# Modulation columns of five groups as GpSimd sums of scaled weight rows instead of 32-column TensorE matmuls

## The chip, the cores and the metric

One core of one Trainium2 chip runs the whole program as one launch. The metric is device time in microseconds (us) from one launch, the median of several runs. The engines named below are TensorE (PE, with its weight loads PEld), VectorE (DVE), ScalarE (ACT), GpSimd (POOL) and SyncE (SP), which issues every DMA of this kernel.

## The reference, cut to what matters

Two transformer layers run over 1024 latent tokens, with 256 context tokens as a prefix. Each layer is steered by modulation columns: a vector-matrix product of a conditioning vector with a weight of 1024 x 6144, once for the latents (`mod`) and once for the context (`mod_c`).

```python
s_c, s_cc = silu(c), silu(c_ctx)
for l in range(2):
    need_ctx = l < 1
    mod   = s_c  @ ada_w[l] + ada_b[l]          # 6144 columns, latents
    mod_c = s_cc @ ada_w[l] + ada_b[l]          # 6144 columns, context
    sh1, sc1, g1, sh2, sc2, g2 = split(mod, 6)  # the same for mod_c
    h  = rms_norm(x,  norm_g[l, 0]) * (1 + sc1) + sh1
    hc = rms_norm(xc, norm_g[l, 0]) * (1 + csc1) + csh1
    y, yc = mixer(h, hc)                        # even: windowed and latent attention
    x = x + g1 * rms_norm(y, norm_g[l, 1])      # odd: normalised and differential attention
    h = rms_norm(x, norm_g[l, 2]) * (1 + sc2) + sh2
    x = x + g2 * rms_norm(swiglu(h), norm_g[l, 3])
    if need_ctx:                                # the context goes through the same steps
        ...
```

In layer 1 the context is normalised for the mixer (which needs `csh1` and `csc1`), and nothing else of `mod_c` is read there.

## The kernel before, in words

Activations lie feature-major: 128 features on the partitions, tokens along the row. Large products are made of float32r matmuls on halves hi and lo of each operand. Work is laid out in program order on a `Recorder`, which stands in place of the engines. At the end `Recorder.issue` lists the instructions anew: an engine that is free in its estimate takes, of the instructions whose operands are there, the first in program order, and a tile is given out ahead of earlier ones only when enough buffers stay free for those (`room`). After that each engine's list is fixed, and the hardware works through each list strictly in order; a wait of one row holds every row behind it on that engine. The scratch tiles are few: 44 of type `T` (128 x 1024), 13 of type `U` (128 x 512), 24 small ones `S`, 8 PSUM banks `b`.

The modulation columns of a layer come in three groups of 2048 columns (g = 0, 1, 2). `g_ada(l, g)` loads the weight in 8 blocks of 128 rows (`kt`), two `T` tiles each. For every block it issues four matmuls (`q`), with the block's 32 columns of `silc` as stationary operand (two of them used, silu(c) and silu(c_ctx), the others zero) and 512 weight columns as moving operand, in float32. Four results of 32 rows share one PSUM bank. Then ScalarE copies the bank, four transposes turn it, and VectorE adds the bias into `mod[l]`; `derive` makes the scales and gates of it.

Group (0, 0) is made at the very start, since the first norm waits for it. The other five are put in a slow queue, `pr.slow`, of which `tick` advances one step per slot of attention. Groups (0, 1), (0, 2), (1, 0) enter at the start of layer 0's attention, groups (1, 1), (1, 2) at the start of layer 1's.

Attention is run by `run_jobs`, slot by slot: a slot is one piece of scores (a PSUM bank), its maximum on VectorE, the exponentials of a piece before on ScalarE (`ex`), and a share of the products with the values (`pv_steps`: transposes, hi and lo copies in two `U` tiles, products). Layer 0 has 352 score pieces: 144 of windowed attention, called A here, then 208 of latent attention, called B. Layer 1 has 192 pieces of differential attention, D, then 192 of normalised attention, C. GpSimd has a part in each. In A and B it adds the two halves of a head pair in `fin` (`T<-T,U`, after a DMA has moved one half), splits the outputs, and copies and adds small columns. In D it combines the two streams of each query tile (`combine`): two products with a factor broadcast along the row (`T<-T,S`) and two sums (`T<-T,T`) of 128 x 512, after which those weights are transposed and multiplied with the values.

The lines that set this:

```python
for q in range(4):
    self.mm(ps[32 * q:32 * q + 32, :], self.silc[:, kt, :],
            ws[kt][q // 2][:, (q % 2) * 512:(q % 2) * 512 + 512], kt == 0, kt == KT - 1)
    yield
# tick():
if self.slow and next(self.slow[0], self) is self:
    self.slow.popleft()
# combine(), on GpSimd:
for h in (slice(0, 512), slice(512, 1024)):
    pr.tt(pb1[:, h], pb1[:, h], f.to_broadcast([P, 512]), ALU.mult, eng=nc.gpsimd)
    pr.tt(pb[:, h], pb[:, h], pb1[:, h], ALU.add, eng=nc.gpsimd)
```

Of the kernel before, what the change touches and what calls it, by code (L numbers as in the profile page):

```python
# [19 lines left out]
P = 128  # L20
D = 1024
# [11 lines left out]
# columns of the packed per-partition parameters  # L33
# [3 lines left out]
# steps from transposed probabilities to their products; slots from differential scores to their weights  # L37
LAG, ALAG, DLAG = 3, 2, 10
# weight tiles split ahead of their products: in layer 0's and layer 1's mixers and output projections
NEAR, ONEAR, N1 = 1, (3, 1), 3  # L40
# time that the pieces of the work beside the matmuls take or wait, us
# [9 lines left out]
class Recorder:  # L51
    """Stands for nc while the program is laid out. The instructions are then issued as a list schedule orders them:
    an engine that is free takes, of the instructions whose operands are there, the first in program order.
    Times are estimates that only decide the order; Tile sets every wait."""
# [26 lines left out]
    @staticmethod  # L81
    def boxes(ap):
        """Tile name and the boxes (rows, columns) that ap covers."""
        shape = ap.tensor.shape
        w = 1
        for s in shape[1:]:
            w *= s
        r0, c0 = divmod(ap.offset, w)
        rows, cols, twice = 1, 1, 0
        for stride, n in ap.ap:  # L90
            if n == 1:
                continue
            if stride >= w:
                rows += (n - 1) * (stride // w)
            elif n == 2 and stride > 512:
                twice = stride
            else:
                cols += (n - 1) * stride
        out = [(r0, r0 + rows, c0, c0 + cols)]
        if twice:  # L100
            out.append((r0, r0 + rows, c0 + twice, c0 + twice + cols))
        return out
# [25 lines left out]
    def record(self, k, f, name, args, kw):  # L128
# [23 lines left out]
        if k == 0:  # L152
            # products into one bank stay in order: a first one marks the whole bank
            t = outs[0].tensor.name
            if t in self.bank:
                deps.add(self.bank[t])
            self.bank[t] = i
        self.ops.append((k, f, name, args, kw, deps, tiles, self.cost(k, name, outs[0], ins, kw), i + self.bias))

    def issue(self):  # L160
# [14 lines left out]
        # from the engine of the row to the engine of the column  # L175
# [87 lines left out]
class FM:  # L263
    """Feature-major activations of one token chunk: [128, KT, n] over 4 KB tiles."""
# [11 lines left out]
class Prog:  # L276
# [41 lines left out]
    def tick(self, us=2.0, wide=1):  # L318
        """Stages of the work under way beside us microseconds of matmuls: one of all short pieces, of the first
        long ones as many as that time has room for, and one of the slow queue.  # L320
        A long piece yields the time that a stage takes, or less than 0 for a time to wait."""
        for g in list(self.bg):
            if next(g, self) is self:
                self.bg.remove(g)
        self.now += us
        self.credit = min(self.credit + us, CAP)
        while self.credit > 0:
            e = next((e for e in list(self.seq)[:wide] if e[1] <= self.now), None)
            if e is None:
                break  # L330
            t = next(e[0], self)
            if t is self:
                self.seq.remove(e)
            elif t < 0:
                e[1] = self.now - t
            else:
                self.credit -= t
        if self.slow and next(self.slow[0], self) is self:
            self.slow.popleft()
# [56 lines left out]
    def split(self, x, hi, lo):  # L396
        """x (float32) into hi + lo, both float32r, exactly."""
        self.nc.scalar.copy(hi, x)
        self.sub(lo, x, f32(hi))
# [4 lines left out]
    def mm3(self, ps, terms):  # L404
        """sum over terms (whi, wlo, xhi, xlo) of w^T x."""
# [6 lines left out]
    def wsplit(self, raw, w=1024):  # L412
        """The first w columns of a weight tile, split."""
        hi, lo = self.T(F32R), self.T(F32R)
        self.split(raw[:, :w], hi[:, :w], lo[:, :w])
        return hi, lo

# [19 lines left out]
    def g_ada(self, l, g, ahead=2):  # L437
        """The 2048 modulation columns of group g."""
# [37 lines left out]
    def derive(self, l, g):  # L476
        """Scales and gates with the norms' gains: A1, G1, A2, G2 per feature and stream."""
        def gain(i):
            c0 = C_NG + (l * 4 + i) * 8
            return self.par[:, c0:c0 + 8].unsqueeze(2).to_broadcast([P, 8, 2])  # L480
        m, dr = self.mod[l], self.der[l]
# [9 lines left out]
    def rstd(self, acc, n, dim, g=1, eng=None):  # L491
        """1/sqrt(mean + eps) per token from the sums acc, each [128, n] (to be added, and over partitions).
        g=2: partitions 0-63 and 64-127 are summed apart. Columns [128 tokens, g] per token tile."""
# [12 lines left out]
        # first guess from the exponent, then three Newton steps  # L506
# [8 lines left out]
    def expand(self, cols):  # L515
        """Columns [128, w], each 64 times in a row."""
# [5 lines left out]
    def bcast(self, cols, g=1):  # L522
        """Token columns [128, nt * g] to rows: [128, n tokens] in PSUM."""
# [8 lines left out]
    def sq_add(self, acc, x, n, k):  # L532
        """x^2, the k-th term, to the sums acc (one on Pool, a second one on DVE)."""
# [17 lines left out]
    def g_modnorm(self, x, n, A, Bv, put, acc=None, w=1):  # L551
        """rms-normalised x times A plus B, split; A(kt), B(kt) are per-partition columns."""
# [20 lines left out]
    def g_residual(self, y, acc, src, G, acc2):  # L573
        """x + G * rms(y), in y's place; x comes from DRAM; its squares' sum goes to acc2."""
# [34 lines left out]
    def load_fm(self, src, c):  # L609
        """src: DRAM [1024 features, tokens of the chunk]."""  # L610
# [16 lines left out]
    def rope(self, q, cos, sin, half, rows=P, n=512):  # L627
        """q [rows, n] float32 in place."""
# [12 lines left out]
    def later(self, f, ticks=2):  # L641
        """f, some ticks later."""
# [8 lines left out]
    def split_out(self, q, dst, c, r0, eng=None, done=None):  # L651
        """q float32 to hi and lo and on to the scratch: dst [rows, 2, tokens], from row r0 on."""
# [20 lines left out]
    def run_jobs(self, jobs):  # L673
        """Slot by slot: one piece of scores, one piece of the step before to its exponentials, and a share
        of the products with the values for the jobs before."""
# [54 lines left out]
class Proj:  # L730
    """Feature-major products with weight tiles that stream through.
    wsrc: DRAM weight tiles [128, KT*M]; order: (tile, chunk) pairs; evac(tile, chunk, psum)."""
# [59 lines left out]
class Job:  # L792
    """One head (or differential head), up to four query tiles.
    passes(si, qi): list of (lhsT, rhs(kind, a, b)) of stream si, kind 'x' or 'c' keys;
    vt(kt): list of (values, 'h' or 'hl' parts of the probabilities, first and last query tile);
    sinks: list of (head, first and last query tile)."""
# [16 lines left out]
    def delay(self):  # L813
        """Slots until the last probabilities are there."""
        return 0 if self.neglam is None else DLAG

    def s_steps(self):
        """Per query tile and stream: score pieces (each returns its maximum's work) and exponentials."""
# [73 lines left out]
    def combine(self, qi, pb1, pc1, s):  # L892
        """p0 - lam z0 / z1 p1, in p0's place: z0 times the differential weights."""
# [15 lines left out]
    def sums(self):  # L909
        """The sums of the exponentials, one column per query tile."""  # L910
# [23 lines left out]
    # windowed  # L934
# [32 lines left out]
    def pcol(self, qi, kt):  # L967
        """probabilities of query tile qi on key tile kt (8, 9: context)."""
# [74 lines left out]
def even_mixer(pr, h, OT, pre_out):  # L1043
    """Layer 0: windowed attention with sinks (A) and latent attention (B), outputs to OT [1024, tokens].
    A generator: first what can be had before the norm."""
# [99 lines left out]
    # latent up-projections  # L1145
# [117 lines left out]
    pr.slow.extend(pr.g_ada(l, g) for l, g in ((0, 1), (0, 2), (1, 0)))  # L1263
# [5 lines left out]
class Pair:  # L1269
    """An even and an odd head that share one 128-row tile of the output: their epilogues.  # L1270
    Products with the values come as [main | low] rows for the even head and [low | main] for the odd one."""
# [10 lines left out]
    def rout(self, c, e=None):  # L1282
        """Where the reciprocal sums of head e (None: of both, context) go."""
# [51 lines left out]
def odd_mixer(pr, h, OT, pre_out):  # L1335
    """Layer 1: normalised grouped attention (C) and differential attention (D), outputs to OT [1024, SEQ].
    A generator: first what can be had before the norm."""
# [5 lines left out]
    # lambda  # L1343
# [79 lines left out]
    # values, token-major  # L1423
# [51 lines left out]
    for hd in range(4):  # L1475
        for c, i0 in (("a", 0), ("b", 4)):
# [30 lines left out]
            elif hd == 0:  # L1507
                loadf = lambda: pr.slow.extend(pr.g_ada(1, g) for g in (1, 2))
# [18 lines left out]
def load_dup(pr, src, r0):  # L1527
    """Keys of one head, hi and lo, each on both halves of the partitions."""
# [15 lines left out]
class OutFFN:  # L1544
    """Output projection, residual, norm, SwiGLU and its residual for the chunks of layer l."""
# [34 lines left out]
    def g_pre(self):  # L1580
        """While attention ends: the first weights, and the attention outputs chunk by chunk."""
# [29 lines left out]
    # SwiGLU, hidden tile by hidden tile  # L1611
# [155 lines left out]
def rope_tables(dim, half):  # L1767
    """cos and signed sin [128, SEQ] for heads of dim rows, two axes, half frequencies each."""
# [22 lines left out]
def columns(w):  # L1791
    """[1024, n*128] to n contiguous tiles [128, KT*128]."""
# [4 lines left out]
def layout(i):  # L1797
    """The inputs in the order in which the kernel reads them."""
# [53 lines left out]
```

## Time and profile before

| | |
|---|---|
| median of 3 runs | 3406.78 us (3404.93 to 3407.7) |
| span of the profiled execution | 3405.7 us, first to last instruction (its time around the span is not on the page) |
| busy: PE, PEld | 3302.8 us (97%), 2687.9 us (79%) |
| busy: DVE, ACT, POOL | 2079.6 us (61%), 1398.0 us (41%), 697.2 us (20%) |
| attention of layer 0 | about 245 us to 740 us of the span |
| attention of layer 1 | about 2060 us to 2545 us |

A busy share is a mean over stages with different limits, and matmuls are pipelined with modelled ends, so PE at 97% is not PE at its peak. All instructions have one source line (L260, the recorder's), so groups are told apart by their tiles: `b` is a PSUM bank, `T<-T,U` an instruction that writes a `T` tile and reads a `T` and a `U` tile.

### The profile page before, as it was taken

The page shows a single profiled execution, that of the slowest core. Times are in us where ns is not written, and L with a number is a line of the kernel's source. Part 1 is how long each engine was busy: PE and PEld are TensorE (multiplying, and loading weights), DVE is VectorE, ACT ScalarE, POOL GpSimd, SP SyncE. Part 2 cuts the span into 40 slices and gives each one's busy share as a digit, 9 for nine tenths or more (in the row PEclk, how much of TensorE's full clock was granted, in tenths as well). Part 3 has the DMA queues.
Part 4 walks back from the last instruction along what each step waited for, and adds up shares of the span by engine and source line. Part 5 has one row for each costly group of instructions (what it writes and reads, how often), then busy time and mean ns, then how long its engine had stood idle before and what let it go on. Part 6 is the DMA issues. An engine that isn't in the chain of part 4 may idle for free.

```text
span 3405.7 us, 45603 instructions
## 1 busy us (share of the span) xinstructions
PE 3302.8 (97%) x16916; PEld 2687.9 (79%) x16916; DVE 2079.6 (61%) x4013; ACT 1398.0 (41%) x3200; POOL 697.2 (20%) x1059
## 2 busy tenths in 40 slices
PE   7989999999999999999998999999999999999997
PEld 5865588887888888888877895678887788888886
DVE  5565588875534444444468745898994545444545
ACT  4365688874411111111134324788994411111111
POOL 2311221125200000000044723682114200000003
PEclk8999999999999999999999999999999999999998
DMA  6266442354201111111123346412145211111111
GB/s 236 81 236 229 167 132 72 98 193 160 80 28 42 44 38 38 38 38 38 38 95 136 105 133 194 130 52 71 60 163 176 68 56 38 56 43 51 56 56 62
DMA packets 134446, 325.56 MB, mean 96 GB/s; under 512 B 12432, under 2 KB 34640, under 8 KB 134224
## 3 DMA queue, kind: packets, MB, share of 16 engines
q1 hardware_dynamic: 134224, 322.65, 28.8%
q8 instruction: 133, 2.18, 0.3%
q14 instruction: 89, 0.73, 0.1%
HBM read 243.63 MB, written 71.63 MB: 93 GB/s over the span
## 4 chain that ended last, share of the span: by engine, by line
PE 82%; DVE 8%; POOL 3%; DMA 3%; ACT 2%; issue 2%; POOLq 0%; SPq 0%; DVEq 0%; ACTq 0%
PE b L260 82%; DVE T L260 3%; DVE U L260 3%; DVE S L260 2%; POOL S L260 2%; POOL U L260 1%; ACT T L260 1%; DMA scr<-T 1%; ACT U L260 1%; DMA T<-in_ada_w_dram 1%; DMA U<-scr 1%; POOL T L260 0%; DMA T<-in_ctxT_dram 0%; POOLq L1847 0%; DMA T<-scr 0%
## 5 line engine op out<-in xcount | busy, mean ns | idle before, releaser
L260 PE MATMUL b<-T,T 128*128 128x512 f32 (+5 forms) x9958 | 2170.5, 367 | 23.1 <-DVE T L260 9.6
L260 PEld LDWEIGHTS b<-T,T 128*128 128x128 f32 (+2 forms) x9958 | 1714.3, 190 | 378.9 <-issue 27.9
L260 PE MATMUL b<-U,T 128*128 128x512 f32 (+2 forms) x3808 | 946.0, 381 | 9.4 <-DVE U L260 4.4
L260 PEld LDWEIGHTS b<-U,T 128*128 128x128 f32 x3808 | 661.6, 190 | 135.6 <-issue 12.8
L260 POOL TENSOR_TENSOR U<-U,U 128x512 f32<-128x512 f32 (+1 forms) x130 | 174.9, 1349 | 1696.5 <-ACT U L260 1692.2
L260 DVE TENSOR_TENSOR T<-T,b 128x512 f32<-128x512 f32 (+1 forms) x872 | 501.6, 631 | 11.4 <-PE b L260 6.5
L260 DVE TENSOR_TENSOR T<-T,T 128x1024 fp32r<-128x1024 f32 (+4 forms) x274 | 316.7, 1170 | 227.3 <-PE b L260 172.9
L260 DVE TENSOR_REDUCE S<-b 128x1 f32<-128x512 f32 (+1 forms) x672 | 377.3, 571 | 116.2 <-PE b L260 111.0
L260 DVE TENSOR_TENSOR U<-U,b 128x512 f32<-128x512 f32 (+1 forms) x118 | 75.2, 637 | 608.4 <-PE b L260 605.5
L260 ACT ACTIVATE T<-b,S 128x512 f32<-128x512 f32 (+1 forms) x640 | 390.6, 616 | 53.5 <-DVE S L260 36.0
L260 ACT CAST T<-T 128x1024 fp32r<-128x1024 f32 (+4 forms) x234 | 225.1, 968 | 360.8 <-PE b L260 296.4
L260 DVE TENSOR_TENSOR U<-b,U 128x512 fp32r<-128x512 f32 (+3 forms) x528 | 335.6, 648 | 21.2 <-ACT U L260 16.8
L260 ACT ACTIVATE U<-b 128x256 f32<-128x256 f32 (+1 forms) x148 | 81.3, 552 | 620.8 <-PE b L260 618.8
L260 ACT CAST U<-b 128x512 fp32r<-128x512 f32 (+3 forms) x528 | 295.7, 572 | 97.4 <-PE b L260 90.4
L260 PE MATMUL b<-ident,T 128*128 128x128 f32 x1968 | 314.3, 276 | 6.3 <-DVE U L260 2.5
L260 PEld LDWEIGHTS b<-ident,T 128*128 128x128 f32 x1968 | 239.7, 141 | 76.0 <-ACT T L260 9.3
L260 ACT CAST U<-U 128x512 fp32r<-128x512 f32 (+1 forms) x110 | 63.6, 578 | 305.1 <-DVE U L260 300.9
L260 POOL TENSOR_TENSOR T<-T,T 128x512 f32<-128x512 f32 (+2 forms) x104 | 132.5, 1282 | 175.6 <-ACT T L260 162.4
L260 PE MATMUL b<-T,silc 128*32 128x512 f32 x384 | 131.8, 626 | 11.0 <-DMA T<-in_ada_w_dram 10.5
L260 DVE TENSOR_TENSOR U<-U,U 128x512 fp32r<-128x512 f32 (+4 forms) x167 | 118.9, 713 | 38.2 <-POOL U L260 27.1
L260 ACT ACTIVATION_READ_ACCUMULATOR T<-b,S 128x1 f32 x640 | 136.6, 213 | 0.0
L260 ACT ACTIVATE U<-T 128x512 f32<-128x512 f32 (+1 forms) x174 | 96.4, 578 | 96.1 <-DVE T L260 90.4
(71 smaller groups left out, 1514.5 us busy)
## 6 DMA issues: line engine op xcount, KB each, us to landing
scr<-T SPq DMA_DIRECT2D x114, 512.0 KB
T<-in_ada_w_dram SPq DMA_DIRECT2D x96, 512.0 KB
T<-in_ffn_in_dram SPq DMA_DIRECT2D x88, 512.0 KB
T<-scr SPq DMA_DIRECT2D x82, 512.0 KB
T<-scr SPq DMA_DIRECT2D x88, 256.0 KB
T<-in_ffn_out_dram SPq DMA_DIRECT2D x44, 512.0 KB
T<-in_w_out_dram SPq DMA_DIRECT2D x32, 512.0 KB
T<-scr SPq DMA_DIRECT2D x72, 128.0 KB
```

The lines of the kernel that those rows point to most:

```text
L260: f(*args, **kw)
```

## The change

Groups (0, 1), (0, 2), (1, 0), (1, 1), (1, 2) are made by a new generator, `g_ada_pool`; group (0, 0) stays with `g_ada`. Each group is made in two halves of 1024 columns. For a half, the 8 weight blocks are loaded into one `T` tile each. GpSimd multiplies each block by its per-partition scalar of `silc` (`TENSOR_SCALAR`, 128 x 512) and adds the products up in an accumulator tile `acc[v]` (`TENSOR_TENSOR`, 128 x 512), for `nv` conditioning vectors: two, or one for groups (1, 1) and (1, 2), whose context columns nothing reads. At the end of a half, 8 float32 products per vector, with 128 columns of `acc[v]` as stationary operand and a column of ones as moving operand, sum over the partitions into one PSUM bank, and VectorE adds the bias. The slow queue advances by one scaled half row block per slot.

```diff
+    def g_ada_pool(self, l, g):
+        nc, d, gp = self.nc, self.d, self.nc.gpsimd
+        nv = 2 if l == 0 or g == 0 else 1
+        m = self.mod[l]
+        for i in range(2):
+            c0 = g * 2048 + i * 1024
+            ws = {}
+
+            def load(kt):
+                if kt < KT:
+                    ws[kt] = self.T()
+                    self.load(ws[kt], d["ada_w"][l, kt * P:(kt + 1) * P, c0:c0 + 1024])
+
+            load(0)
+            load(1)
+            yield
+            acc = [self.T() for _ in range(nv)]
+            for kt in range(KT):
+                w = ws.pop(kt)
+                for v in range(nv):
+                    sc = self.silc[:, kt, v:v + 1]
+                    for h in (slice(0, 512), slice(512, 1024)):
+                        if kt:
+                            t = self.U()
+                            self.ts(t, w[:, h], sc, eng=gp)
+                            self.tt(acc[v][:, h], acc[v][:, h], t, ALU.add, eng=gp)
+                        else:
+                            self.ts(acc[v][:, h], w[:, h], sc, eng=gp)
+                        yield
+                load(kt + 2)
+            yield
+            ps = self.b()
+            for q in range(8):
+                for v in range(nv):
+                    self.mm(ps[:, 2 * q + v:2 * q + v + 1], acc[v][:, q * P:(q + 1) * P], self.ones[:, 0:1], True, True)
+            c1 = g * 16 + i * 8
+            pv = ps[:, 0:16].rearrange("p (q v) -> p q v", v=2)[:, :, 0:nv]
+            bv = self.par[:, C_AB + l * 48 + c1:C_AB + l * 48 + c1 + 8].unsqueeze(2).to_broadcast([P, 8, nv])
+            self.add(m[:, c1:c1 + 8, 0:nv], pv, bv)
+        self.derive(l, g, nv)
...
-    pr.slow.extend(pr.g_ada(l, g) for l, g in ((0, 1), (0, 2), (1, 0)))
+    pr.slow.extend(pr.g_ada_pool(l, g) for l, g in ((0, 1), (0, 2), (1, 0)))
...
-                loadf = lambda: pr.slow.extend(pr.g_ada(1, g) for g in (1, 2))
+                loadf = lambda: pr.slow.extend(pr.g_ada_pool(1, g) for g in (1, 2))
```

`derive` takes `nv` and works on so many columns; the other differences are comments.

How the lists change is seen at three places. The first is GpSimd's list where layer 0's attention begins. `S_538` is a small column of the first job; `U_452` a tile of the latent projections. Before:

```order
L260 TENSOR_TENSOR U_452<-U_452,T_113 128x512
L260 COPY S_538<-S_537 128x4
L260 COPY S_756<-par 128x4
L260 TENSOR_TENSOR S_538<-S_538 128x4
L260 COPY U_608<-S_512 128x256
```

Now, with `T_545` and `T_546` the two accumulators of the first half and `T_542`, `T_543` its first weight blocks:

```order
L260 TENSOR_TENSOR U_452<-U_452,T_113 128x512
L260 TENSOR_SCALAR T_545<-T_542,silc 128x512 x2
L260 TENSOR_SCALAR T_546<-T_542,silc 128x512 x2
L260 TENSOR_SCALAR U_560<-T_543,silc 128x512
L260 TENSOR_SCALAR U_566<-T_543,silc 128x512
L260 TENSOR_TENSOR T_545<-T_545,U_560 128x512
L260 TENSOR_TENSOR T_545<-T_545,U_566 128x512
L260 TENSOR_SCALAR U_568<-T_543,silc 128x512
L260 TENSOR_SCALAR U_571<-T_543,silc 128x512
L260 TENSOR_TENSOR T_546<-T_546,U_568 128x512
L260 COPY S_538<-S_537 128x4
L260 TENSOR_TENSOR T_546<-T_546,U_571 128x512
```

The job's own copy now stands behind eleven large instructions of the new kind. In all, 360 such instructions (192 `TENSOR_SCALAR`, 168 `TENSOR_TENSOR`) stand in GpSimd's list between the start of layer 0's attention and its score piece 221, with 98 of the attention's own between them.

The second place is TensorE's list in layer 0. Before, in A, rows with `silc` stand singly between score products (`T_877,T_878`, `T_875,T_878`, `T_876,T_878`) and transposes of weights (`ident`):

```order
L260 MATMUL b_975<-T_956,silc 32x512
L260 MATMUL b_983<-T_877,T_878 128x256 x2
L260 MATMUL b_975<-T_957,silc 32x512 x2
L260 MATMUL b_984<-T_875,T_878 128x384
L260 MATMUL b_984<-T_876,T_878 128x384
L260 MATMUL b_986<-T_877,T_878 128x256 x2
```

Now, in B, the sums of the sixth and last half of layer 0 (`b_1811`, accumulators `T_1599` and `T_1600`) stand between score products and transposes, near score piece 221:

```order
L260 MATMUL b_1896<-T_1658,T_1656 128x512
L260 MATMUL b_1896<-T_1659,T_1656 128x512
L260 MATMUL b_1896<-T_1658,T_1657 128x512
L260 MATMUL b_1897<-ident,T_1834 128x128
L260 MATMUL b_1897<-ident,T_1848 128x128
L260 MATMUL b_1897<-ident,T_1861 128x128
L260 MATMUL b_1897<-ident,T_1882 128x128
L260 MATMUL b_1811<-ones,T_1600 128x1
L260 MATMUL b_1811<-ones,T_1599 128x1
```

The rows with `silc`, the last of which stood near score piece 100, are gone; the rows with `ones` wait for GpSimd's last addition into their accumulator, and stand near the pieces 46, 74, 109, 143, 185 and 221, one half each.

The third place is GpSimd's list in D. Before, the four large instructions of `combine` follow one another query tile by query tile, with nothing but a small copy between:

```order
L260 TENSOR_TENSOR T_4200<-T_4200,S_4194 128x512 x2
L260 TENSOR_TENSOR T_4195<-T_4195,T_4200 128x512 x2
L260 COPY S_4172<-S_4219 128x1
L260 TENSOR_TENSOR T_4231<-T_4231,S_4219 128x512 x2
L260 TENSOR_TENSOR T_4220<-T_4220,T_4231 128x512 x2
```

Now, with `T_4423` an accumulator and `T_4479`, `T_4487` weight blocks:

```order
L260 TENSOR_TENSOR T_4473<-T_4473,S_4452 128x512 x2
L260 TENSOR_TENSOR T_4453<-T_4453,T_4473 128x512 x2
L260 TENSOR_SCALAR U_4488<-T_4479,silc 128x512
L260 TENSOR_SCALAR U_4492<-T_4479,silc 128x512
L260 TENSOR_TENSOR T_4423<-T_4423,U_4488 128x512
L260 TENSOR_TENSOR T_4423<-T_4423,U_4492 128x512
L260 TENSOR_SCALAR U_4497<-T_4487,silc 128x512
L260 TENSOR_SCALAR U_4499<-T_4487,silc 128x512
L260 TENSOR_TENSOR T_4423<-T_4423,U_4497 128x512
L260 TENSOR_TENSOR T_4423<-T_4423,U_4499 128x512
L260 COPY S_4466<-S_4489 128x1
L260 TENSOR_TENSOR T_4500<-T_4500,S_4489 128x512 x2
```

Between two query tiles' combinations stand eight rows of the new kind. All 120 of layer 1 (64 `TENSOR_SCALAR`, 56 `TENSOR_TENSOR`) stand before score piece 74 of D's 192, with 68 of D's own rows; the four halves' rows with `ones` stand near D's pieces 15, 33, 53 and 73.

## Rows read from the trace of the kernel before

**Rows 1.** The page: busy time, and two of the rows in 40 slices.

```profile
PE 3302.8 (97%) x16916; PEld 2687.9 (79%) x16916; DVE 2079.6 (61%) x4013; ACT 1398.0 (41%) x3200; POOL 697.2 (20%) x1059
...
PE   7989999999999999999998999999999999999997
...
PEclk8999999999999999999999999999999999999998
```

**Rows 2.** Windows: length; busy (count) of PE, PEld, DVE, ACT, POOL; PEclk; DMA share; GB/s.

```profile
246.50:561.00 314.50, 304.73 (x1695) 212.31 (x1696) 217.95 (x650) 225.69 (x686) 65.75 (x105) 0.98 0.54 170
561.00:737.00 176.00, 174.40 (x1062) 149.29 (x1061) 147.87 (x306) 146.09 (x386) 27.10 (x30) 1.00 0.37 111
2062.50:2172.00 109.50, 106.74 (x432) 49.65 (x432) 71.60 (x184) 59.24 (x171) 57.16 (x69) 0.98 0.63 195
2180.00:2310.00 130.00, 127.09 (x668) 97.69 (x668) 127.31 (x313) 107.53 (x303) 111.54 (x163) 0.97 0.22 68
```

**Rows 3.** The same windows, matmuls on silc alone: length; PE busy (count); PEclk; DMA; GB/s.

```profile
246.50:561.00 314.50, 69.19 (x192) 0.98 0.54 170
...
2062.50:2172.00 109.50, 46.33 (x128) 0.98 0.63 195
```

**Rows 4.** Timeline of PE: first matmuls on silc beside either attention.

```profile
246.53 1.05 PE L260 MATMUL b<-T,silc 128*32 128x512 f32 x4 [0.48 <-PE b L260]
...
2062.48 1.05 PE L260 MATMUL b<-T,silc 128*32 128x512 f32 x2
```

**Rows 5.** Lines of ACT by form, 240 to 561.2 us: count | busy us, mean ns | idle.

```profile
L260 ACT ACTIVATE T<-b,S 128x256 f32<-128x256 f32 x111 | 54.6, 492 | 5.5 <-DVE S L260 5.5
...
L260 ACT ACTIVATE T<-b,S 128x512 f32<-128x512 f32 x47 | 32.7, 699 | 2.8 <-DVE S L260 2.4
L260 ACT ACTIVATE T<-T,S 128x384 f32<-128x384 f32 x48 | 30.3, 631 | 5.4 <-DVE S L260 5.2
...
L260 ACT ACTIVATE T<-T,S 128x256 f32<-128x256 f32 x16 | 8.4, 524 | 0.1
```

**Rows 6.** The same, 2060 to 2172 us.

```profile
L260 ACT ACTIVATE T<-b,S 128x512 f32<-128x512 f32 x50 | 34.1, 690 | 24.2 <-PE b L260 14.6 <-DVE S L260 8.7 <-POOL T L260 0.9
...
L260 ACT ACTIVATE T<-b,S 128x256 f32<-128x256 f32 x12 | 5.8, 480 | 0.1
L260 ACT ACTIVATE U<-b,S 128x256 f32<-128x256 f32 x12 | 5.8, 480 | 3.8 <-DVE S L260 3.8
```

**Rows 7.** Lines of POOL by form, 246.5 to 561 us.

```profile
L260 POOL COPY U<-S 128x512 f32<-128x512 f32 x10 | 6.1, 611 | 14.0 <-PE b L260 13.8 <-DVE mod L260 0.2
```

**Rows 8.** The same, 2062.5 to 2172 us.

```profile
L260 POOL TENSOR_TENSOR T<-T,T 128x512 f32<-128x512 f32 x22 | 28.5, 1310 | 0.0
L260 POOL TENSOR_TENSOR T<-T,S 128x512 f32<-128x512 f32 x22 | 23.3, 1077 | 11.8 <-DVE S L260 4.0 <-ACT T L260 3.6 <-PE b L260 2.1
```

**Rows 9.** Timeline of POOL in D: start, duration, instruction.

```profile
2181.11 2.52 POOL L260 TENSOR_TENSOR T<-T,T 128x512 f32<-128x512 f32 x2
2183.59 0.20 POOL L260 TENSOR_TENSOR S<-S 128x4 f32<-128x4 f32 x1
```

**Rows 10.** Waits of POOL, 246.5 to 561 us: total, times, longest.

```profile
POOL T L260 <- DMA T<-U: 70.5, 16, 13.4
POOL T L260 <- ACT T L260: 46.5, 13, 8.4
```

**Rows 11.** Lines of PE by form, whole span.

```profile
L260 PE MATMUL b<-T,silc 128*32 128x512 f32 x384 | 131.8, 626 | 11.0 <-DMA T<-in_ada_w_dram 10.5 <-PE b L260 0.5
...
L260 PE MATMUL b<-ones,U 128*128 128x1 f32 x288 | 42.3, 268 | 18.9 <-POOL U L260 16.1 <-DVE U L260 2.4
```

**Rows 12.** Windows in A, columns as in Rows 2.

```profile
280.00:300.00 20.00, 15.54 (x84) 9.47 (x82) 9.61 (x34) 11.03 (x34) 3.37 (x7) 0.89 0.33 108
300.00:320.00 20.00, 19.44 (x73) 10.93 (x74) 8.79 (x28) 9.36 (x28) 3.69 (x6) 0.85 1.02 348
```

More of the change, by code (lines that the diff above doesn't have):

```diff
@@ L474, in g_ada, with derive @@
         self.derive(l, g)
-    def derive(self, l, g):
+    def g_ada_pool(self, l, g):
[36 more added lines that the diff above has]
+        self.derive(l, g, nv)
+    def derive(self, l, g, nv=2):
         def gain(i):
             c0 = C_NG + (l * 4 + i) * 8
-            return self.par[:, c0:c0 + 8].unsqueeze(2).to_broadcast([P, 8, 2])
-        m, dr = self.mod[l], self.der[l]
+            return self.par[:, c0:c0 + 8].unsqueeze(2).to_broadcast([P, 8, nv])
+        m, dr = self.mod[l][:, :, 0:nv], self.der[l][:, :, :, 0:nv]
         if g == 0:
```

## The prediction

> **What bounds the kernel now.** I read the page first. TensorE is busy in 97% of the span and at nine tenths or more in almost every slice, at the full clock; GpSimd is at 20% [rows 1]. From that alone, work taken from TensorE and given to GpSimd looks like a gain. A mean share says nothing of a stretch, though, so I next cut the span into the stretches in which the change works. While the three groups of layer 0 run, from the first `silc` matmul at 246.5 us [rows 4] to about 561 us, TensorE is busy 304.7 of 314.5 us and GpSimd 65.8 us; in D, from 2062.5 us to 2172 us, TensorE 106.7 of 109.5 us and GpSimd 57.2 us [rows 2]. The reader should see in the last two windows of those rows that the stretches behind have no slack to give back: from 561 us TensorE is busy 174.4 of 176 us, and in the rest of D VectorE is busy 127.3 of 130 us. The ends 561 and 2172 us were chosen from the new lists: there 221 and 73 score pieces are through (222 exponentials by 561.2 us, 74 by 2172 us, one per piece) [rows 5, 6], and near those pieces the last sums of each layer now stand.
>
> **What is removed.** The `silc` matmuls take 69.2 us of TensorE's time in layer 0 and 46.3 us in D [rows 3], 115.5 us together. That is the most the change can gain. The loads of the weights move the same bytes, 512 KB a tile, and SyncE's list has as many rows as before. The 20 transposes and 5 copies that also go are priced at nothing: they stand in the same full TensorE time, and only lower the rival below by a few us. In exchange TensorE gets 128 sums over partitions (three groups of two halves with 16, two groups of two halves with 8). A float32 product leaves two rows in the trace (6 groups of 32 products on `silc` are 384 rows), and a row with one column of ones took 42.3 / 288 = 0.147 us [rows 11], so they cost 256 x 0.147 = 38 us.
>
> **What is added on GpSimd.** The trace has two-input additions of 128 x 512 there: 1.31 us each, and 1.24 us from start to start when two follow one another [rows 8, 9], since neighbours overlap slightly. I take 1.25 us. It has no `TENSOR_SCALAR` of that size. Below stands the copy of a broadcast column to 128 x 512, one input, 0.61 us [rows 7]; above, the product with a factor broadcast along the row, which runs as a two-input instruction, 1.08 us [rows 8]. A product with a per-partition scalar streams one input, like the copy, so I take 0.61 us and keep both ends. In sentences apart: the Trainium skill, GPSIMD Engine Reference, section 3.1, gives a body with one input stream 1.03 cycles an element at 1.2 GHz, which is an estimate of 0.44 us for 512, and holds GpSimd to be the wrong place for elementwise work; no run here shows the 0.44. By that figure the forecast would come down by 256 x 0.17 = 44 us, with the same sign.
>
> Layer 0 has 192 products and 168 additions: 192 x 0.61 + 168 x 1.25 = 117 + 210 = 327 us. Layer 1 has 64 and 56: 39 + 70 = 109 us.
>
> **Where that lies.** GpSimd is idle for 314.5 - 65.8 = 249 us in layer 0's stretch and 52 us in D's, so 327 and 109 us don't fit. Whether that matters depends on who waits. Two things tie attention to GpSimd. Its list is one line in strict order, with the attention's own additions, copies and `combine` rows between the new ones, and the sums stand in TensorE's list near fixed score pieces, each behind GpSimd's last addition. So TensorE can't pass piece 221 before GpSimd has worked off its list up to there. Nor can attention run far ahead in between: the 13 `U` tiles are shared with the hi and lo halves of the probabilities.
>
> Layer 0: GpSimd starts when the first weights have landed, taken as 246.5 us, where TensorE starts now [rows 4]. It has the 327 us and its 98 rows of attention. The window holds 105 such rows in 65.8 us [rows 2]; without seven of the larger ones I take 60 us. It comes to the end at 246.5 + 387 = 633.5 us, where the kernel before is at 561: 72.5 us lost. Layer 1: 2062.5 + 109 + 57 (68 of the window's 69 rows) = 2228.5 us against 2172: 56.5 us lost.
>
> To this come GpSimd's own waits. In layer 0 it waited 16 times, 4.4 us on average, for the DMA that moves half of a head pair, and 13 times, 3.6 us, for ScalarE [rows 10]. These waits don't vanish, they are only covered by the new rows between: 360 rows over 98 are 3.7 to each, some 3.3 us. That leaves 16 x 1.1 + 13 x 0.3 = 21 us; I take 20, with 0 and the full 117 us as ends, the lower far likelier. In D the combination's inputs come ahead of need when GpSimd is late, so I take 0.
>
> **The sum.** 72.5 + 56.5 + 20 = 149 us on a span of 3405.7 us gives 3555 us; the median shown stands 1.1 us above the span, less than the rounding here. The removal of 115.5 us isn't subtracted: it falls in stretches where TensorE will be waiting. What is late next is everything behind `combine` in D (transposes and products of the weights) and, in A, the outputs and the `U` tiles.
>
> **Rivals.**
> First, *the products cost as the broadcast form does*: 1.08 instead of 0.61 us for 256 of them, 120 us more, 3675 us. For it: the scalar comes from memory, as the broadcast factor does. Against: that form is a `TENSOR_TENSOR` and reads two streams.
>
> Second, on the other side, *GpSimd keeps up, and TensorE's time is the gain*: 3407 - 115.5 + 38 = 3329 us. That needs the new rows to fit in GpSimd's idle time. It decides at 249 / 360 = 0.69 us a row in layer 0 (D: 52 / 120 = 0.44 us), where I count 0.91. For it: the page's 20%. Against: the additions alone, at 1.25 us, fill 210 of the 249 us and more than all of D's.
>
> Third, *TensorE's clock falls while it waits*. In the window from 280 us it was busy 15.5 of 20 us, and there and in the next window the granted clock had a mean of 0.89 and 0.85 [rows 12], so part of each was at 1.2 GHz instead of 2.4. If the whole of layer 0's stretch ran so, its 304.7 - 69.2 = 235.5 us would double to 471 and pass GpSimd's 387: 84 us more, 3639 us. D's 60.4 us would double to 121, still under 166. Against it as a whole: the waits here are spread, a few us each. The Trainium skill has a rule beside this, TensorE: Matmul & The Clock Gate, Part 1: an idle array falls to half its clock, and a busy one gets it back. The two windows agree.
>
> **How the numbers follow.** The forecast, GpSimd setting the pace with one-input products, has a chance of 0.68; its own range is 3505 to 3600 (0.57 us a product and no waits below, twice the waits and some clock above). The dear products have 0.14, the fallen clock 0.08, the gain 0.06. The remaining 0.04 are for a loss that is much smaller, or nil, because attention runs ahead where I say it can't. The range from 3480 to 3670 holds the forecast and the clock case whole and the dear products' lower part; the gain and a small loss lie outside. Within 0.2% (about 7 us, what a measurement of this kernel can tell from no change) I give 0.02, faster 0.06, slower 0.92.
>
> **What the profile after would show.** GpSimd's busy time up by some 436 us, to about 1130 us, and nine tenths or more of it in the slices from 246 to 640 us and from 2062 to 2230 us. Additions of 1.25 to 1.3 us and products near 0.6 us; products of 1.05 us or more mean the first rival. The last `ones` matmul of layer 0 near 640 to 655 us. TensorE's waits for GpSimd's `T` tiles long in A, and its busy share down there; the stretches behind as long as before. If TensorE stays at nine tenths through A and the sums wait for nothing, the pace argument is wrong, and the second rival is right. A granted clock near one half through A would show the third.

## The result, and the profile after

The changed kernel takes 3757.13 us (median of 4 runs, 3756.66 to 3758.82) against 3405.99 us: the ratio is 1.1035, 95% interval 1.1021 to 1.1048, 351 us slower. The direction and the mechanism were forecast; the loss is more than twice the forecast 149 us, and lies outside the range.

The page of the changed kernel, lines as in [rows 1] with GpSimd's slices added:

```profile
PE 3364.2 (90%) x16832; PEld 2794.4 (74%) x16832; DVE 2119.9 (56%) x4003; ACT 1399.6 (37%) x3195; POOL 1359.6 (36%) x1539
...
PE   7985566789999999999999997559999999999997
...
POOL 2359999971251000000014555998411410000002
PEclk8996667799999999999999998669999999999998
```

TensorE's row sinks to five and six tenths in the slices from about 280 us to 660 us, where GpSimd's stands at nine; the granted clock sinks with it. The same picture, narrower, stands from about 2350 us to 2530 us, in D. The stretches that answer to [rows 2] end where the same score pieces are through, told by the ends of ScalarE's exponentials, one per piece: the 222nd of layer 0 ends at 799.0 us (before: 561.6), the last, 352nd, at 982.7 (737.6); D's 74th ends at 2501.8 (2172.4), its last, 192nd, at 2650.7 (2300.9). Columns: length; busy time and count of PE, PEld, DVE, ACT, POOL; granted clock; DMA share; GB/s.

```profile
246.50:798.00 551.50, 363.56 (x1649) 288.06 (x1649) 221.14 (x638) 225.35 (x681) 546.22 (x448) 0.71 0.32 95
799.00:982.70 183.70, 181.39 (x1096) 155.83 (x1095) 149.20 (x310) 147.07 (x390) 39.66 (x43) 0.98 0.38 113
2300.00:2501.00 201.00, 101.69 (x395) 72.56 (x394) 96.78 (x184) 59.76 (x173) 201.00 (x171) 0.67 0.37 114
2501.80:2650.70 148.90, 130.71 (x669) 100.98 (x669) 132.33 (x307) 106.40 (x302) 129.22 (x179) 0.92 0.20 60
```

The stretch to score piece 221 lasts 551.5 us instead of 314.5. The third window begins with GpSimd's first new product for D, at 2299.8 us; from D's first exponential to its 74th it is 192.8 us, instead of 108.0 before. GpSimd is busy 546.2 of the 551.5 us and all of the 201. The stretches behind give nothing back and lose a little more: 183.7 us after, 176.0 before, behind piece 222, and 148.9 after, 128.5 before, in the rest of D. GpSimd's last new addition ends at 804.1 us in layer 0 and at 2519.8 us in layer 1, so its work reaches 5 and 18 us into them. In all, layer 0's attention ends 245.1 us later, and D takes 105.2 us more.

Who waited in layer 0's stretch (total us, times, longest), GpSimd first, then the others for GpSimd:

```profile
POOL U L260 <- PE b L260: 2.0, 1, 2.0
POOL T L260 <- PE b L260: 0.9, 1, 0.9
...
DVE S L260 <- POOL S L260: 105.7, 26, 11.7
...
ACT U L260 <- POOL T L260: 88.6, 23, 11.1
...
DVE U L260 <- POOL T L260: 60.5, 28, 6.1
...
PE b L260 <- POOL T L260: 24.7, 7, 4.9
```

GpSimd's own waits are all but gone. VectorE waits 105.7 us for small columns `S` from GpSimd (0.3 us in the same stretch before); 71.4 us of that are 12 waits for the attention's own copies of 128 x 4, which stand in GpSimd's list behind the new rows. ScalarE and VectorE wait 88.6 and 60.5 us to write `U` tiles (3.0 and none before); 84.3 and 51.4 us of that end with a new addition, `T<-T,U` of 128 x 512, which frees its `U` tile. TensorE itself waits only 24.7 us for GpSimd's `T` tiles, all of it in the sums.

GpSimd's own instructions, by form (count, then busy us and mean ns):

```profile
L260 POOL TENSOR_SCALAR U<-T,silc 128x512 f32<-128x512 f32 x224 | 349.0, 1567 | 3.0 <-PE b L260 2.0
L260 POOL TENSOR_TENSOR T<-T,U 128x512 f32<-128x512 f32 x224 | 281.5, 1273 | 0.0
...
L260 POOL TENSOR_TENSOR T<-T,S 128x512 f32<-128x512 f32 x64 | 67.0, 1061 | 1.1 <-ACT T L260 1.1
```

The reader should stop at the first of these. The product with a `silc` column takes 1567 ns, more than an addition with two inputs (1273 ns) and more than `combine`'s product in broadcast form (1061 ns). Its time is much the same throughout (ns min/median/max over both layers). The 68 products that no VectorE instruction overlaps have a median of 1564 ns, the 56 that VectorE overlaps for over nine tenths of their time one of 1565, so contention with VectorE doesn't make it dear:

```profile
L260 POOL TENSOR_SCALAR U<-T,silc x224: 1554/1564/1744, 245.6 to 2518.3; 128x512 f32<-128x512 f32 x112
```

From start to start, in the timeline:

```profile
403.19 3.12 POOL L260 TENSOR_SCALAR U<-T,silc 128x512 f32<-128x512 f32 x2
406.26 2.50 POOL L260 TENSOR_TENSOR T<-T,U 128x512 f32<-128x512 f32 x2
408.72 1.58 POOL L260 TENSOR_SCALAR U<-T,silc 128x512 f32<-128x512 f32 x1
```

Two products take 3.07 us, two additions 2.46 us, so a product costs 1.54 us and an addition 1.23 us. The last sums of layer 0 on TensorE stand near 800 us, not near 640 to 655 us as forecast, and most of them in the full stretch behind piece 222:

```profile
797.06 0.38 PE L260 MATMUL b<-ones,T 128*128 128x1 f32 x2 [1.81 <-POOL T L260]
...
802.62 1.95 PE L260 MATMUL b<-ones,T 128*128 128x1 f32 x16 [0.40 <-POOL T L260]
...
805.64 2.80 PE L260 MATMUL b<-ones,T 128*128 128x1 f32 x14
```

### The profile page after: what moved, and what is told of

Its sections match the earlier page's. It is cut to its first block, busy times and chain, and to the rows that moved or that the text cites. A ratio compares the mean times of both kernels' runs of the same rounds, so it can differ in the third digit from the quotient of the medians.

```text
span 3755.4 us, 46012 instructions
## 1 busy us (share of the span) xinstructions
PE 3364.2 (90%) x16832; PEld 2794.4 (74%) x16832; DVE 2119.9 (56%) x4003; ACT 1399.6 (37%) x3195; POOL 1359.6 (36%) x1539
## 5 line engine op out<-in xcount | busy, mean ns | idle before, releaser
L260 PE MATMUL b<-T,T 128*128 128x512 f32 (+5 forms) x9958 | 2212.1, 372 | 60.9 <-ACT T L260 21.2
L260 PEld LDWEIGHTS b<-T,T 128*128 128x128 f32 (+2 forms) x9958 | 1743.7, 193 | 388.4 <-ACT T L260 43.3
L260 PE MATMUL b<-U,T 128*128 128x512 f32 (+2 forms) x3808 | 987.6, 390 | 65.8 <-ACT U L260 29.6
L260 PEld LDWEIGHTS b<-U,T 128*128 128x128 f32 x3808 | 682.8, 195 | 198.3 <-ACT U L260 45.8
L260 PE MATMUL b<-ident,T 128*128 128x128 f32 x1968 | 350.3, 298 | 130.0 <-ACT T L260 46.3
L260 POOL TENSOR_TENSOR T<-T,U 128x512 f32<-128x512 f32 (+2 forms) x288 | 355.0, 1246 | 183.5 <-DMA T<-U 148.9
L260 PEld LDWEIGHTS b<-ident,T 128*128 128x128 f32 x1968 | 262.0, 153 | 197.4 <-ACT T L260 57.0
L260 DVE TENSOR_TENSOR U<-b,U 128x512 fp32r<-128x512 f32 (+3 forms) x528 | 334.6, 647 | 123.8 <-POOL T L260 60.5
L260 POOL TENSOR_SCALAR U<-T,silc 128x512 f32<-128x512 f32 x224 | 349.0, 1567 | 3.0 <-PE b L260 2.0
```

The lines of the kernel that those rows point to most:

```text
L260: f(*args, **kw)
```

## Experiments

Three questions were put to the chip: whether the price of the product is the whole error, what ties attention to GpSimd, and where such work would fit. Each run has the kernel before beside it on the same chip (medians 3406.08 and 3405.01 us, within about 1 us of the one above).

**The product in broadcast form.**

```diff
-                            self.ts(t, w[:, h], sc, eng=gp)
+                            self.tt(t, w[:, h], sc.to_broadcast([P, 512]), ALU.mult, eng=gp)
```

(The first block's product, straight into the accumulator, likewise.)

> The changed kernel, with each product on GpSimd written as a TENSOR_TENSOR with the silc column broadcast along the row, the form that combine has (1.05 us from start to start), in place of TENSOR_SCALAR (1.54 us in the trace after). Theory (the product's price on a saturated GpSimd is the whole of the error): 256 x 0.49 = 125 us less than the changed kernel, 3632 us, within 15 us. Rival (TensorE at the lower clock sets the pace of the stretch): nothing changes by over 20 us, 3735 us or more.

3633.58 us (median of 4), ratio 1.0672 (1.0654 to 1.0689), 123.6 us less than the changed kernel. By form and by window up to about score piece 221:

```profile
L260 POOL TENSOR_TENSOR U<-T,silc 128x512 f32<-128x512 f32 x224 | 230.5, 1047 | 4.6 <-PE b L260 3.6
```

```profile
246.50:704.00 457.50, 334.52 (x1653) 264.65 (x1653) 219.85 (x639) 224.63 (x681) 445.91 (x449) 0.79 0.38 113
```

The product's price falls as expected and the time follows it within 2 us. GpSimd is still busy 445.9 of 457.5 us, and the stretch is 94 us shorter, which is 192 x 0.49 us: it follows GpSimd's price. TensorE's clock, at a mean of 0.79 of full speed, is still low, and isn't the pace in this form either.

**A constant as the scalar of half of the products.**

```diff
-                            self.ts(t, w[:, h], sc, eng=gp)
+                            self.ts(t, w[:, h], sc if h.start else 0.5, eng=gp)
```

> The changed kernel, with a constant 0.5 as the scalar of every product on the first 512 columns of a tile; the other 512 keep the silc column, so half of the modulation columns are not those of the reference. It prices the scalar from memory against the operation, side by side in one trace. Theory (reading the scalar from memory makes the product dear): the constant form takes about 0.6 us, the other 1.57 us, and the time falls by 128 x 0.94 = 120 us, to 3637 us. Rival (TENSOR_SCALAR is dear at this size whatever its scalar): both forms 1.57 us, 3757 us.

3746.62 us in one run. Both forms in one trace:

```profile
L260 POOL TENSOR_SCALAR U<-T,silc 128x512 f32<-128x512 f32 x112 | 176.0, 1572 | 0.7
L260 POOL TENSOR_SCALAR U<-T 128x512 f32<-128x512 f32 x112 | 167.3, 1493 | 2.1 <-PE b L260 1.7
```

The theory fell, the rival holds: with a constant the product takes 1493 ns, hardly less. Not the scalar's place makes it dear but the operation itself, at this size, on this engine; why it does stays open.

**Only layer 0's groups on GpSimd.**

```diff
-                loadf = lambda: pr.slow.extend(pr.g_ada_pool(1, g) for g in (1, 2))
+                loadf = lambda: pr.slow.extend(pr.g_ada(1, g) for g in (1, 2))
```

> The changed kernel, with groups (1,1) and (1,2) made by matmuls again; the three groups of layer 0 stay on GpSimd. Theory (each stretch loses by its own GpSimd work, 245 us in layer 0 and 105 us in D): 3757 - 105 = 3652 us, with D as long as before. Rival (part of D's loss is carried over from layer 0, through tiles or the clock): more than 3670 us.

3651.82 us (median of 4), ratio 1.0723 (1.0705 to 1.074). The two stretches lose apart: 245.8 us belong to layer 0 and 105.3 us to D. From D's first exponential to its 74th it is 109.2 us, against 108.0 before; the window of D's first 73 pieces:

```profile
2304.00:2417.00 113.00, 109.28 (x445) 51.97 (x444) 72.81 (x181) 58.75 (x171) 57.05 (x69) 0.98 0.63 197
```

**The sums 80 slots later.** The body of the sums becomes a generator of its own, which waits 80 slots:

```diff
-            ps = self.b()
+            def sums(i=i, acc=acc):
+                for _ in range(80):
+                    yield
+                ps = self.b()
...
+            self.bg.append(sums())
```

> The changed kernel, with the sums over partitions of each half put 80 slots later in program order; everything on GpSimd stays. Theory (attention is held by GpSimd's list itself: its own rows stand in line behind the new ones, and U tiles are freed late): no change over 30 us, 3727 to 3790 us. Rival (TensorE is held by the sums that wait in its list): attention runs on while GpSimd is late, and D's loss and most of layer 0's go; under 3600 us.

3767.03 us in one run. TensorE's waits, and the window:

```profile
PE b L260 <- DVE U L260: 54.5, 30, 7.2
PE b L260 <- ACT T L260: 54.2, 28, 10.0
PE b L260 <- DVE S L260: 46.7, 17, 8.2
PE b L260 <- ACT U L260: 22.6, 30, 3.8
PE b L260 <- POOL U L260: 9.3, 4, 3.6
```

```profile
246.50:798.00 551.50, 360.31 (x1613) 284.43 (x1613) 219.94 (x635) 224.74 (x681) 549.07 (x451) 0.71 0.31 93
```

The row `PE b <- POOL T` of the changed kernel is gone: TensorE no longer waits for an accumulator on GpSimd. The stretch is as long as in the changed kernel, with GpSimd busy 549.1 of 551.5 us. So the prediction's statement that the sums hold TensorE was a bound that happened to be right, not the cause. What holds attention is GpSimd's list itself, through the rows of attention in it and the `U` tiles: VectorE still waits 99.6 us for GpSimd's `S` columns, and ScalarE and VectorE 65.2 and 53.2 us to write `U` tiles; TensorE sees that as waits for VectorE and ScalarE. Which of these two carries more was not tried.

**The price that the prediction assumed.** Each product is replaced by a copy:

```diff
-                            self.ts(t, w[:, h], sc, eng=gp)
+                            gp.tensor_copy(t, w[:, h])
```

(`Recorder.cost` prices this copy as it priced the product, so that the list stays the same.)

> The changed kernel, with each product on GpSimd replaced by a plain copy of the weights, so the five groups' columns are unscaled sums of weights. It puts the price that the prediction assumed (0.61 us) in place of the measured 1.54 us and leaves the rest of the sum to be tested. Theory (everything else in the sum holds, without the 20 us of waits): 256 x 0.93 = 238 us less than the changed kernel, 3519 us, 113 us above the kernel before. Rival (an instruction of this size costs 1.5 us on GpSimd whatever it does with one tensor): 3757 us.

3558.09 us in one run, 39 us more than expected here, and 3 us from the forecast 3555. The copy, the window and GpSimd's waits in it:

```profile
L260 POOL COPY U<-T 128x512 f32<-128x512 f32 x224 | 132.9, 615 | 26.0 <-PE b L260 24.8
```

```profile
238.00:656.00 418.00, 330.79 (x1676) 265.51 (x1676) 227.81 (x661) 233.14 (x708) 374.20 (x458) 0.84 0.44 133
```

```profile
POOL U L260 <- PE b L260: 27.1, 16, 5.8
POOL T L260 <- PE b L260: 12.0, 3, 5.9
```

The copy takes 615 ns, within 1% of the prediction's 0.61 us. GpSimd is no longer full (374.2 of 418 us), and waits some 39 us for TensorE, by way of tiles that are freed late. The waits that the prediction put at 20 us are there as soon as GpSimd isn't saturated, somewhat larger and for another engine. The clock's mean is 0.84 in this window, so part of these waits may be the clock's; that was not tried apart.

**The products on VectorE.**

```diff
-                            self.ts(t, w[:, h], sc, eng=gp)
+                            self.ts(t, w[:, h], sc)
```

> The changed kernel, with the products on VectorE (TENSOR_SCALAR, 0.43 us for 128 x 512 in the trace before) and only the additions on GpSimd. Theory (the loss is GpSimd's total): GpSimd in layer 0's stretch 208 + 60 = 268 us of 314, no longer the pace, VectorE 218 + 83 = 301 us; in D GpSimd 69 + 57 = 126 us of 109, about 17 us lost; together 3390 to 3425 us. Rival (the rows of GpSimd and VectorE hold each other up where both read SBUF): 3450 us or more.

3527.97 us (median of 4), ratio 1.0356 (1.034 to 1.0371); a miss, on the rival's side. VectorE's products (ns min/median/max), two rows of its timeline, the window up to score piece 221 (the 222nd exponential ends at 644.9 us), and GpSimd's longest wait in it, in total:

```profile
L260 DVE TENSOR_SCALAR U<-T,silc x224: 447/891/2387, 250.6 to 2277.9; 128x512 f32<-128x512 f32 x112
L260 DVE TENSOR_SCALAR T<-T,silc x32: 471/480/1581, 238.9 to 2241.7; 128x512 f32<-128x512 f32 x32
```

```profile
360.41 1.37 DVE L260 TENSOR_SCALAR U<-T,silc 128x512 f32<-128x512 f32 x1
...
369.00 0.47 DVE L260 TENSOR_SCALAR T<-T,silc 128x512 f32<-128x512 f32 x1
```

```profile
246.50:645.00 398.50, 326.88 (x1685) 272.37 (x1685) 356.73 (x834) 230.45 (x685) 291.22 (x273) 0.81 0.44 134
```

```profile
POOL T L260 <- DVE U L260: 32.1, 48, 5.6
```

Of the 256 products in this trace, the 33 that no GpSimd instruction overlaps take 471 to 487 ns; the 129 that GpSimd overlaps for over nine tenths of their time have a median of 923 ns, up to 1910. VectorE is busy 356.7 of 398.5 us, instead of the 301 expected, and is the busiest engine; that it alone sets the pace is not shown. The Trainium skill has the rule, SBUF — State Buffer, Who interferes with whom: VectorE's second pair of ports is GpSimd's only one, an exclusive lock, and a `tensor_scalar` on VectorE can take it. The spread between these two groups agrees.

**Three groups beside the FFN.** Groups (0, 1) and (0, 2) stay matmuls; groups (1, 0), (1, 1), (1, 2) go to GpSimd while layer 0's FFN runs, in broadcast form, in pieces of 512 columns held in `U` tiles.

```diff
-    pr.slow.extend(pr.g_ada_pool(l, g) for l, g in ((0, 1), (0, 2), (1, 0)))
+    pr.slow.extend(pr.g_ada(l, g) for l, g in ((0, 1), (0, 2)))
...
         self.p2.run((KT - 3, self.begin))
+        if self.l == 0:
+            pr.slow.extend(pr.g_ada_ffn(1, g) for g in range(3))
```

> Groups (0,1) and (0,2) by matmuls beside layer 0's attention, as before; groups (1,0), (1,1), (1,2) on GpSimd beside layer 0's FFN, where GpSimd idles, in pieces of 512 columns in U tiles, with the broadcast product. Theory (what matters is whether GpSimd has room in the stretch): 8 sums of 512 x 1024 x ... on GpSimd are 8 x (32 products and additions at about 1.15 us) = 280 us in some 800 us; TensorE loses 23 + 46 us of silc matmuls and gains 128 rows of ones at 0.147 us, 19 us; 3406 - 50 = 3356 us. Rival (VectorE's additions with two SBUF inputs in the FFN are held up by GpSimd, or U tiles run short): no gain or a loss, 3400 us or more.

3382.32 us (median of 4), ratio 0.9934 (0.9917 to 0.995), 23 us faster than the kernel before. Windows of layer 0's stretch, of the FFN and of D's first 73 pieces (from 1.9 us ahead of D's first exponential, as in [rows 2]), GpSimd's product, and VectorE's splits of weights in the FFN, here and in the kernel before:

```profile
246.50:561.00 314.50, 290.28 (x1669) 216.62 (x1670) 221.08 (x657) 229.35 (x701) 66.93 (x106) 0.96 0.48 146
880.00:1700.00 820.00, 817.75 (x4333) 706.75 (x4332) 402.51 (x649) 142.84 (x215) 313.46 (x255) 1.00 0.22 69
2069.70:2141.30 71.60, 61.85 (x296) 43.86 (x294) 69.94 (x173) 56.96 (x170) 55.89 (x69) 0.98 0.31 79
```

```profile
L260 POOL TENSOR_TENSOR U<-U,silc 128x512 f32<-128x512 f32 x128 | 150.1, 1179 | 350.6 <-DMA U<-in_ada_w_dram 186.2 <-DVE U L260 73.8 <-PE b L260 50.1
```

```profile
L260 DVE TENSOR_TENSOR T<-T,T 128x1024 fp32r<-128x1024 f32 x59 | 84.9, 1439 | 83.4 <-PE b L260 81.7
...
L260 DVE TENSOR_TENSOR T<-T,T 128x1024 fp32r<-128x1024 f32 x60 | 73.5, 1225 | 90.5 <-PE b L260 86.2 <-ACT T L260 2.6
```

D's first 73 pieces take 71.6 us instead of 109.5 [rows 2]: here 38 of TensorE's 46 us come back. VectorE is busy 69.9 of the 71.6 us, where it was busy 71.6 of 109.5: with the `silc` matmuls gone it is all but full, so little more could come. The rest of D takes 134.0 us instead of 128.5, so D as a whole gains 33 us. The other half of the expected 50 us didn't come: layer 0's attention ends only 7 us sooner, though 23 us of `silc` matmuls are gone from it (why was not tested). From its end to D's first exponential it takes 1340.8 us instead of 1326.8. TensorE is as full as ever there (817.8 of 820 us in the FFN), so its sums, 19 us by the expectation, are nearly paid in full. VectorE's splits, which read two SBUF tiles, take 1439 ns, against 1225 in the kernel before: the 30 that no GpSimd instruction overlaps take at most 1227 ns, the other 29 have a median of 1720.

**All five groups on GpSimd, spread.** As the one above, and groups (0, 1), (0, 2) in broadcast form, two or three slots to a step, over layer 0's attention.

```diff
-                        yield
+                        for _ in range(2 + v):
+                            yield
```

> As the kernel with the three groups in the FFN, and groups (0,1), (0,2) also on GpSimd, with the broadcast product and spread over almost all 352 slots of layer 0's attention (2 or 3 slots to a step). Theory: GpSimd has 273 + 93 = 366 us of work in a stretch of 490 us, so it fits; TensorE loses another 46 us and gains 19 us: 3329 us, up to 3350 us if A is still paced by GpSimd. Rival (beside attention any large work on GpSimd delays its rows): more than the kernel with the FFN groups alone, 3370 us or more.

3383.96 us (median of 4), ratio 0.9937 (0.9922 to 0.9952): no gain over the version with the FFN groups alone, as the rival has it, but no clear loss against it either. Layer 0's stretch:

```profile
246.50:561.00 314.50, 277.33 (x1652) 231.42 (x1652) 227.71 (x664) 235.00 (x718) 251.90 (x274) 0.94 0.45 131
```

In a window of the same length TensorE is busy 277.3 us and GpSimd 251.9, against 290.3 and 66.9 above. The removed matmuls shorten A: its 144th exponential ends at 441.3 us, against 452.9 with the FFN groups alone. The B behind it loses that again: 291.7 us against 277.9. That GpSimd's steps delay its rows there was not tested.

## Why the prediction was wrong

- *TensorE's 97% is no sign of a gain, and the stretches behind have no slack.* Right, they give nothing back. They aren't as long as before, though: 183.7 us against 176.0 behind piece 222, 148.9 against 128.5 in the rest of D. In the lists all of layer 1's new rows stand ahead of D's piece 74; on the chip 83 of D's exponentials were through when the last new addition ended.
- *Attention runs at GpSimd's pace.* Right: 546.2 us busy of 551.5. Of the ties that it names, the sums in TensorE's list aren't the one that acts (late sums: no change), and the forecast sign, long waits of TensorE for GpSimd's `T` tiles in A, came to only 24.7 us in layer 0's stretch. The strict list and the `U` tiles are left, and VectorE's and ScalarE's waits show both.
- *An addition costs 1.25 us.* Right: 1.23 us from start to start. Most of the 128 sums fall where TensorE waits, and what they cost there doesn't show; the last 30 rows of layer 0 (1.95 and 2.80 us) stand in a full stretch.
- *A product costs 0.61 us, "like the copy", between 0.61 and 1.08.* **This step failed.** It measured 1.54 us, above the upper end. The step took the form with one tensor input to be the cheap one and the broadcast form as a bound above it; it is the other way round (1567 against 1061 ns). The term was 117 + 39 us and is 192 x 1.54 + 64 x 1.54 = 394 us: 238 us too small. The first rival named the right term, but its 0.47 us more for a product are half of the measured 0.93.
- *GpSimd's waits, 20 us.* 2.9 us in the layer 0 stretch, since it never ran dry. It also began 8.6 us sooner there, its first product starting at 237.9 us, and some 7 us sooner in D (2299.8 us, where 2062.5 answers to 2307). 149 + 238 - 20 + 3 - 9 - 7 = 354 us, against 351 measured; the last 3 us are not accounted for.
- *With a product of 0.61 us the sum gives 3555 us.* The copy's run, with 615 ns, took 3558 us. The agreement is partly luck: up to piece 222 GpSimd began 8.6 us sooner and was busy 374 us instead of the forecast 387, but was idle 44 us instead of 20; and layer 0's attention lost 100 us where the sum has 92.5, D 51 us where it has 56.5.
- *The clock.* It did fall, to a mean of 0.71 in the layer 0 stretch, between its levels of 1.2 and 2.4 GHz; but GpSimd had 5 us of idle time there, so by that the clock can't have cost more there.

The range failed with the same step: both of its ends for the product came from instructions of another operation, and nothing in the trace bounded `TENSOR_SCALAR` from above. The lower end of the forecast's own range, 3505 us, doesn't follow from its reason either: without the 20 us of waits and with 0.57 us a product the sum gives 3525.

## What to carry to other kernels

Before work is moved to an idle engine, count the stretch in which it will run, not the span: 360 rows didn't fit into 249 idle us at any price above 0.69 us a row, and three groups of the same work beside the FFN did fit. Price an operation by itself at its own size; fewer inputs don't bound it, and a small form (0.2 us at 4 columns) tells nothing of the slope. Rows that are put into the list of an engine that becomes full by them delay every row behind them there, and with those the engines that need them: here VectorE waited 105.7 us for small columns that cost GpSimd 0.2 us each.

## What was not expected of the hardware

On GpSimd a `TENSOR_SCALAR` of 128 x 512 float32 takes 1567 ns with a column as scalar and 1493 ns with a constant, a `TENSOR_TENSOR` with a broadcast column 1047 ns, a copy 615 ns, a two-tensor addition 1273 ns. The Trainium skill, GPSIMD Engine Reference, section 4.1, has one-input operations roughly at line rate; the copy comes nearest to that, at half the price of the two-tensor addition, this operation costs more than that addition, and here the measurement decides. On VectorE the same product went from 471 to 487 ns without GpSimd beside it to a median of 923 ns beside a GpSimd that is mostly adding, and a split of 128 x 1024 with two SBUF inputs from 1227 ns at most to a median of 1720.
